# Hybrid decoder layer on one core: mixing loads one step later, chunks begun four units later, down operands four steps ahead

## The chip, the cores and the metric

The kernel runs on one core of a Trainium2 chip. The metric is the device time of one execution in microseconds (us), the median of the runs shown.

## What is computed

One decoder layer, float32, for 2048 positions of width 1024: token mixing, then an MLP of hidden width 4096, each between two RMS norms and added to its input.

```python
S, H = 2048, 4                     # one input; 4 attention heads, 4 mLSTM heads
h = rmsnorm(x, g_mix_pre)
dq, dk, dv, mq, mk, mv, mo, mi, mf = split(h @ w_in)
for blk in range(S // 128):        # differential attention, per head, causal
    s = q[2 maps, 128 rows of blk] @ k[2 maps, all keys up to blk]  # rotary before
    p = softmax(s); p = p[0] - lam * p[1]
    out[blk] = p @ v[keys up to blk]
# mLSTM, recurrent over chunks of positions, per head, with state C and norm n
scores = (qc @ kc.T) * decay_matrix
num = w_inter * (qc @ C) + scores @ vc
C = decay * C + (w * kc).T @ vc
mixed = concat(rmsnorm(attention), rmsnorm(mlstm) * sigmoid(mo)) @ w_out
x = x + rmsnorm(mixed, g_mix_post)
u = square(relu(rmsnorm(x, g_mlp_pre) @ w_up))
return x + rmsnorm(u @ w_down, g_mlp_post)
```

## The kernel before

Five stages follow one another: the input projections (to 560 us), mixing (to 1045), the output projection (to 1300), the up product (to 1880) and the down product (to 2503). A float32 product is made of three matmuls on operands split into a high and a low part. Results of a stage that the next one needs go through DRAM: Kd, Qd and Vd (keys, queries, values), mqkd, Md, Wd, mvd and mod (the mLSTM's inputs), od (the mixed heads), ud (the activations).

**Mixing.** A unit is one head and one block of 128 rows (`units`, 64 of them, 16 to a head). `scores` (L564 on) makes the scores of a unit on PE (L585), DVE adds the mask and finds maxima (L589), ACT takes exponentials (L598); `values` transposes the probabilities (L664), multiplies by V (L669), and DVE scales the result into `o` (L671). After each fourth unit `head_norm` (L675 on) normalises `o` on POOL and ACT and stores it to od by a DMA on POOL's queue (L687). `o` has two places, so that a group's store must have landed before the group after the next writes. K and Q are loaded two units ahead of the unit whose scores are being made, which is itself up to four units ahead (`ahead`); V is loaded two units ahead of `values`.

The mLSTM runs in 16 chunks of 128 positions, each with three stages that are put between the units: `chunk_scores` (transposes L738, scores L747, weighting by E on DVE L749), `chunk_values` (L764, L765, state update L771) and `chunk_norm` (L796 and its store). A chunk has five loads (`chunk_load`: qk, E, two halves of wb, vaug) and a sixth, its gate mog (`chunk_gate`). `chunk_weights` prepares E on POOL and ACT (L725, L727) and wb on POOL (L729). The loop over the units puts the 48 stages in proportion to the work of the units passed. Before: chunks 0 and 1 are loaded and chunk 0 prepared ahead of the loop, later chunks are loaded at the end of `chunk_values` two chunks back.

All these loads go through `load` (L530): SP issues them in the order in which they are written, since `tc.keep_in_program_order` pins the kept instructions of a queue among themselves. A DMA issue waits in SP's queue until the place that it fills is free. Everything that is not kept is ordered by a scheduler at build time.

**The down product.** Seven products of half-size blocks stand for eight (`DOWN_ORDER` 1, 6, 5, 3, 2, 7, 4). Each takes 16 steps; a step is 24 matmuls into eight PSUM banks `pd` (L1034). The operands of a step are made in `operands`: activations `ar` (load L1251), split into `ao` (ACT L1253, DVE L1228), and weights `br` (load L1234), for products 5, 6, 7 and 4 combined out of two to four tiles by DVE (`right`, L1228), then split into `bo` (ACT L1257, DVE L1228). There are 4 places of `ar`, 6 of `ao`, 10 of `br` and 7 of `bo`. At the end of a product `take` copies or adds a bank into `y`; the next product's matmul into that bank waits for it.

Of the kernel before, what the change touches and what calls it, by code (L numbers as in the profile page):

```python
# [15 lines left out]
ALU = mybir.AluOpType  # L16
# [6 lines left out]
NT = 16  # L23
# [9 lines left out]

UP_ORDER = (1, 2, 6, 7, 5, 3, 4)
DOWN_ORDER = (1, 6, 5, 3, 2, 7, 4)
NEAR = (1, 2, 6, 7)

SHAPES = {
# [464 lines left out]
def phase_mix(tc, a, sc, ident, late):  # L503
    nc = tc.nc
    with ExitStack() as ctx:
# [138 lines left out]
        op = pool("op", 2)  # L644
# [5 lines left out]

        def values(u, pd, rz):
            h, qb = units[u]
            load_ahead(1, u + 2)
            if qb % 4 == 0:
                outs[h] = op.tile([128, 4, 128], F32, name="o")
            o = outs[h]
            nb = qb + 1
            pv = psV.tile([128, 128], F32, name="pv")
            for j in range((nb + 3) // 4):
                m = min(4, nb - 4 * j)  # L660
                tp = psT.tile([128, 512], F32, name="tp")
                for i in range(m):
                    b = 4 * j + i
                    nc.tensor.transpose(tp[:, i * 128:(i + 1) * 128], pd[:, b * 128:(b + 1) * 128], ident)  # L664
                pT = ptp.tile([128, 512], F32, name="pT")
                nc.scalar.copy(pT[:, :m * 128], tp[:, :m * 128])
                for i in range(m):
                    b = 4 * j + i
                    nc.tensor.matmul(pv, pT[:, i * 128:(i + 1) * 128], Vs[h, j][:, i, :],  # L669
                                     start=(b == 0), stop=(b == nb - 1))  # L670
            nc.vector.tensor_scalar(o[:, qb % 4, :], pv, rz[:, 0:1], None, op0=ALU.mult)  # L671
            if qb % 4 == 3:
                head_norm(h, qb // 4, o)
# [55 lines left out]
            keep(nc.gpsimd.tensor_tensor(wb, m["qk"][:, 0:2, :], wb, op=ALU.mult))  # L729

        def chunk_scores(c):
            if c + 1 < NT:
                chunk_weights(c + 1)
            m = ms[c]
            qk = m["qk"]
            ktp = psM.tile([128, 512], F32, name="m")
# [16 lines left out]
        def chunk_values(c):  # L753
# [13 lines left out]
            if c < NT - 1:  # L767
                up = psM.tile([128, 512], F32, name="m")
                for h in range(H):
                    hp, r = (h % 2) * 64, h // 2  # L770
# [3 lines left out]
                    nc.vector.scalar_tensor_tensor(C[:, r], C[:, r], dec2[:, r, c:c + 1],  # L774
                                                   up[:, r * 130:(r + 1) * 130], op0=ALU.mult, op1=ALU.add)
            m["ns"] = ns
            if c + 2 < NT:
                chunk_load(c + 2)

        def chunk_norm(c):  # L780
            m = ms.pop(c)
# [8 lines left out]
            for h in range(H):  # L790
# [7 lines left out]
            nc.gpsimd.dma_start(  # L798
                sc["od"][c // 4][c % 4 * 128:c % 4 * 128 + 128, 512:1024].rearrange("p (h v) -> p h v", h=4), mog)
            if c + 2 < NT:  # L800
                chunk_gate(c + 2)

        stages = [chunk_scores, chunk_values, chunk_norm]
        for c in range(2):
            chunk_load(c)
            chunk_gate(c)
        chunk_weights(0)
        N = len(units)
        total = sum(qb + 2 for _, qb in units)
        seen, stage = 0, 0  # L810
        for u in range(N):
            ahead(u)
            seen += units[u][1] + 2
            while stage * total < seen * 48 and stage < 48:
                stages[stage % 3](stage // 3)
                stage += 1
            if u == N - 1:
# [383 lines left out]
def mlp_down(tc, a, sc, out):  # L1201


    nc = tc.nc
    with ExitStack() as ctx:
# [21 lines left out]
        def tt(out, x, y, op):  # L1227
            nc.vector.tensor_tensor(out, x, y, op=op)  # L1228

        def right(i, j):  # L1230
            def load(r, c):
                t = br()
                fb = 2 * j + r - 1
                nc.sync.dma_start(t, a["w_down"][fb * 128:(fb + 1) * 128, (c - 1) * 512:c * 512])  # L1234
                return t

            if i in (1, 2, 3):
                return load(*{1: (1, 1), 2: (2, 1), 3: (2, 2)}[i])
            x, y = load(*((1, 2) if i == 5 else (2, 2))), load(*((1, 1) if i == 5 else (1, 2)))
            tt(x, x, y, ALU.subtract)  # L1240
            if i in (6, 4):
                z = load(1, 1)
                tt(x, x, z, ALU.add)
            if i == 4:
                z = load(2, 1)
                tt(x, z, x, ALU.subtract)
            return x

        def operands(i, j):
# [61 lines left out]
                    nc.vector.scalar_tensor_tensor(t, t, rr, x1[:, sl], op0=ALU.mult, op1=ALU.add)  # L1311
                nc.sync.dma_start(out[rows, sl], t)

        TAIL = 6
        for i in DOWN_ORDER:
            first, last = i in (1, 2, 7), i in (3, 2, 4)
            n = 16 - (TAIL if i == DOWN_ORDER[-1] else 0)
            for j in range(n):
                l, r = operands(i, j)
                for b in range(8):  # L1320
                    step(i, b, l, r, first and j == 0, last and j == 15)
                    if j == 15:
                        take(i, b)
                if i == 7 and j % 2 == 0:
                    load_x1(j // 2, 1)
                    sumsq(j // 2, 1, 1)
                    sumsq(j // 2, 1, 2)
                    finish(j // 2, 1)
                if i == 4 and j < 8:
                    sumsq(j, 2, 2)  # L1330
                if i == 4 and j < 5:
                    load_x1(j, 2)
            if n < 16:
                lr = [operands(i, j) for j in range(n, 16)]
                for b in range(8):
                    for j in range(n, 16):
                        step(i, b, *lr[j - n], False, last and j == 15)
                    take(i, b)
                    sumsq(b, 2, 1)
                    finish(b, 2)  # L1340
                    if b < 3:
                        load_x1(b + 5, 2)


def _constants():
# [62 lines left out]
```

## Time and profile before

| | |
|---|---|
| median of 3 runs | 2508.93 us (2505.14, 2508.93, 2512.16) |
| the profiled execution | 2512.56 us, span 2510.8 us |
| PE busy | 2426.9 us, 97% of the span |
| DVE, ACT, POOL busy | 1467.3, 1061.3 and 468.2 us |
| granted TensorE clock, mean | 0.983 |

A row of the windows view gives the busy time of each engine in a stretch and the clock that PE was granted there (1.00 is 2.4 GHz, 0.50 is 1.2 GHz). In a timeline row the bracket tells how long the engine stood idle before the instruction and what released it. The chain of waits lists the pieces of work, in order of time, on which the end of the program hung. PE is the engine that the other engines feed, so what counts is where PE is idle or slow.

### The profile page before, as it was taken

Reading aid. Unit: us, or ns where it says so; the run is one execution under the profiler, and the core shown is the slowest. Engines: PE = TensorE matmul, PEld = TensorE weight load, DVE = VectorE, ACT = ScalarE, POOL = GpSimd, SP = SyncE. Lnnn points to the kernel's source line nnn. Section 1 sums busy time; section 2 is a strip of 40 time slices with the busy share of each in tenths; the row PEclk is TensorE's granted clock in tenths of the full one; section 3 lists DMA queues with packets and bytes.
Section 4 is the critical chain, followed back from the end, with each engine's and each line's share of the span. In section 5 each row is a group of like instructions: output and inputs, shape, how many; then the busy total and the mean of one; then the engine's idle time right before and its main releaser. Section 6 shows DMA issues by size and latency. Waiting matters only on the chain.

```text
span 2510.8 us, 34565 instructions
## 1 busy us (share of the span) xinstructions
PE 2426.9 (97%) x12030; PEld 2032.6 (81%) x12030; DVE 1467.3 (58%) x3132; ACT 1061.3 (42%) x2103; POOL 468.2 (19%) x756
## 2 busy tenths in 40 slices
PE   8999999998999998999989999999999999999998
PEld 6888889996877787878768888888888888887886
DVE  4474441115887887466676666676664543333885
ACT  7210112324876776544443443443443332332433
POOL 0002222202755646423210000000000000000323
PEclk9999999997999999999999999999999999999999
DMA  9323333226564564255784446734457764444883
GB/s 323 131 76 101 111 112 93 60 84 154 143 139 130 118 153 109 73 179 190 236 316 149 165 150 253 293 140 150 160 200 280 239 206 161 150 150 159 301 284 138
DMA packets 288559, 424.35 MB, mean 169 GB/s; under 512 B 23584, under 2 KB 162224, under 8 KB 286848
## 3 DMA queue, kind: packets, MB, share of 16 engines
q1 hardware_dynamic: 285472, 413.55, 51.3%
q0 software_dynamic: 2912, 8.59, 1.1%
q8 instruction: 95, 1.56, 0.3%
q14 instruction: 80, 0.66, 0.1%
HBM read 283.56 MB, written 138.49 MB: 168 GB/s over the span
## 4 chain that ended last, share of the span: by engine, by line
PE 80%; DVE 8%; DMA 7%; issue 2%; ACT 2%; POOL 1%; SPq 1%; POOLq 0%; DVEq 0%; ACTq 0%
PE pd L1034 16%; PE A L1034 14%; PE B L1034 10%; PE pp L93 7%; PE pp L95 7%; PE pp L94 7%; PE pv L669 4%; DMA br<-in_w_down_dram 4%; PE s L585 4%; PE tp L664 2%; PE po L93 1%; PE po L95 1%; PE po L94 1%; PE m L765 1%; DMA t<-in_x_dram 1%
## 5 line engine op out<-in xcount | busy, mean ns | idle before, releaser
L1034 PE MATMUL pd<-bo,ao 128*128 128x512 f32 x2688 | 614.4, 391 | 6.9 <-DVE y L1228 5.3
L1034 PEld LDWEIGHTS pd<-bo,ao 128*128 128x128 f32 x2688 | 506.3, 189 | 114.8 <-issue 5.0
L1034 PE MATMUL A<-B,w 128*128 128x512 f32 x1536 | 364.8, 393 | 9.8 <-DVE w L1104 4.8
L1034 PEld LDWEIGHTS A<-B,w 128*128 128x128 f32 x1536 | 290.2, 189 | 74.3 <-ACT w L1134 6.9
L93 PE MATMUL pp<-w,xT 128*128 128x512 f32 (+1 forms) x768 | 271.5, 359 | 8.7 <-ACT w L230 7.7
L94 PE MATMUL pp<-w,xT 128*128 128x512 f32 (+1 forms) x768 | 273.1, 356 | 0.0
L1034 PE MATMUL B<-B,w 128*128 128x512 f32 x1152 | 272.2, 389 | 0.0
L95 PE MATMUL pp<-w,xT 128*128 128x512 f32 (+1 forms) x768 | 271.3, 355 | 0.0
L1286 POOL TENSOR_TENSOR y<-y,g 128x512 f32<-128x512 f32 x32 | 49.2, 1561 | 1153.2 <-ACT jk L1280 1089.2
L1034 PEld LDWEIGHTS B<-B,w 128*128 128x128 f32 x1152 | 216.1, 188 | 45.7 <-ACT w L1134 0.9
L1253 ACT CAST ao<-ar 128x1024 fp32r<-128x1024 f32 x112 | 117.7, 1052 | 294.6 <-PE pd L1034 158.7
L1228 DVE TENSOR_TENSOR ao<-ar,ao 128x1024 fp32r<-128x1024 f32 x112 | 139.1, 1243 | 168.0 <-ACT ao L1253 164.3
L1104 DVE TENSOR_TENSOR w<-wr,w 128x512 fp32r<-128x512 f32 x224 | 152.2, 688 | 123.0 <-ACT w L1134 121.7
L585 PE MATMUL s<-K,Q 128*128 128x512 f32 (+3 forms) x640 | 187.0, 405 | 17.3 <-DVE p L589 8.8
L1134 ACT CAST w<-wr 128x512 fp32r<-128x512 f32 x224 | 136.9, 620 | 116.6 <-PE B L1034 106.4
L598 ACT ACTIVATE p<-p,nm 128x128 f32<-128x128 f32 (+15 forms) x128 | 153.8, 1202 | 47.7 <-DVE nm L597 38.2
L669 PE MATMUL pv<-V,pT 128*128 128x128 f32 x1088 | 154.5, 286 | 11.4 <-DVE o L671 8.7
L93 PEld LDWEIGHTS pp<-w,xT 128*128 128x128 f32 x768 | 144.4, 188 | 25.3 <-ACT w L230 8.6
L669 PEld LDWEIGHTS pv<-V,pT 128*128 128x128 f32 x1088 | 142.4, 198 | 22.7 <-DVE o L671 10.0
L95 PEld LDWEIGHTS pp<-w,xT 128*128 128x128 f32 x768 | 144.5, 188 | 15.2
L94 PEld LDWEIGHTS pp<-w,xT 128*128 128x128 f32 x768 | 144.6, 188 | 15.1 <-DVE w L231 0.3
L589 DVE TENSOR_SCALAR_CACHE_REDUCE p<-s 128x512 f32<-128x512 f32 x192 | 129.5, 683 | 28.4 <-PE s L585 22.5
(260 smaller groups left out, 3604.4 us busy)
## 6 DMA issues: line engine op xcount, KB each, us to landing
ud<-u SPq DMA_DIRECT2D x224, 256.0 KB, 2.4
ar<-ud SPq DMA_DIRECT2D x112, 512.0 KB, 3.9
br<-in_w_down_dram SPq DMA_DIRECT2D x224, 256.0 KB, 4.0
wr<-in_w_up_dram SPq DMA_DIRECT2D x128, 256.0 KB, 3.4
Bd<-hl SPq DMA_DIRECT2D x40, 512.0 KB, 4.1
B<-Bd SPq DMA_DIRECT2D x10, 2048.0 KB, 13.3
Q<-Qd SPq DMA_DIRECT2D x128, 128.0 KB, 4.9
raw<-in_xT_dram SPq DMA_DIRECT2D x32, 256.0 KB, 5.0
```

The source lines that it names most:

```text
L93: nc.tensor.matmul(ps, lhs[0], rhs[0], start=first, stop=False)
L94: nc.tensor.matmul(ps, lhs[0], rhs[1], start=False, stop=False)
L95: nc.tensor.matmul(ps, lhs[1], rhs[0], start=False, stop=last)
L585: nc.tensor.matmul(ps[:, :w], Q[:, var, c, qo:qo + 128], Ks[h, j][:, c, 0:w], start=(var == 0), stop=(var == 1))
L589: nc.vector.tensor_scalar(dst, ps[:, :w], 0.0, None, op0=ALU.add, op1=ALU.max, accum_out=mx[:, c, j:j + 1])
L598: nc.scalar.activation(pc[:, :W], pc[:, :W], AF.Exp, bias=nm[:, c:c + 1], accum_out=Z[:, c:c + 1])
L669: nc.tensor.matmul(pv, pT[:, i * 128:(i + 1) * 128], Vs[h, j][:, i, :], start=(b == 0), stop=(b == nb - 1))
L1034: nc.tensor.matmul(ps, l[i], r[j], start=(first and k == 0 and m == 0), stop=(last and k == n - 1 and m == 2), skip_group_check=True)
L1104: self.nc.vector.tensor_tensor(out, x, y, op=op)
L1134: self.nc.scalar.copy(w[:, 0], src)
L1228: nc.vector.tensor_tensor(out, x, y, op=op)
L1253: nc.scalar.copy(l[:, 0], u)
```

## The change

In mixing, V is loaded one unit ahead of `values` where it was two; a chunk's five loads move from the end of `chunk_values` to the end of `chunk_norm` of two chunks back; `chunk_weights` of the next chunk moves from the start of `chunk_scores` to the end of `chunk_values`. The loads of chunks 0 and 1 move into the loop, to units 1 and 3, with the preparation of chunk 0 at unit 3, and the first chunk stage comes four units later (the first four units are 2 + 3 + 4 + 5 = 14 of the 608 that `total` counts). In the down product the operands are made four steps ahead in the written program (in the last product's tail six, as before), and DVE's combinations of `br` tiles are kept in written order.

```diff
         def values(u, pd, rz):
-            load_ahead(1, u + 2)
+            load_ahead(1, u + 1)
...
         def chunk_scores(c):
-            if c + 1 < NT:
-                chunk_weights(c + 1)
...
             m["ns"] = ns
-            if c + 2 < NT:
-                chunk_load(c + 2)
+            if c + 1 < NT:
+                chunk_weights(c + 1)
...
             if c + 2 < NT:
+                chunk_load(c + 2)
                 chunk_gate(c + 2)
...
-        for c in range(2):
-            chunk_load(c)
-            chunk_gate(c)
-        chunk_weights(0)
...
             ahead(u)
             seen += units[u][1] + 2
-            while stage * total < seen * 48 and stage < 48:
+            if u in (1, 3):
+                chunk_load(u // 2)
+                chunk_gate(u // 2)
+            if u == 3:
+                chunk_weights(0)
+            while stage * (total - LEAD) < (seen - LEAD) * 48 and stage < 48:
                 stages[stage % 3](stage // 3)
...
+        def keep(out, x, y, op):
+            tc.keep_in_program_order(nc.vector.tensor_tensor(out, x, y, op=op))
...
-            tt(x, x, y, ALU.subtract)
+            keep(x, x, y, ALU.subtract)
             if i in (6, 4):
                 z = load(1, 1)
-                tt(x, x, z, ALU.add)
+                keep(x, x, z, ALU.add)
             if i == 4:
                 z = load(2, 1)
-                tt(x, z, x, ALU.subtract)
+                keep(x, z, x, ALU.subtract)
...
+        TAIL, AHEAD = 6, 4
+        steps = [(i, j) for i in DOWN_ORDER for j in range(16)]
+        made = []
+        for n, (i, j) in enumerate(steps):
+            tail = n == len(steps) - TAIL
+            while len(made) < min(n + (TAIL if tail else AHEAD + 1), len(steps)):
+                made.append(operands(*steps[len(made)]))
...
-                l, r = operands(i, j)
                 for b in range(8):
-                    step(i, b, l, r, first and j == 0, last and j == 15)
+                    step(i, b, *made[n], first and j == 0, last and j == 15)
```

Three places show what this moves. The lines of the changed kernel are two higher in mixing (L532 for L530) and two to five higher in the down product (L1230 for L1228, L1233 for the kept combinations).

On SP's queue, where mixing begins, before (Kd_64 and Qd_68 hold the keys and queries that units 4 and 5 are the first to read; the two Q groups of four are one tile for units 4 and 5 and one for 6 and 7):

```order
L692 DMA masks<-in_c_masks_dram 128x128
L530 DMA qk<-mqkd 128x4x128
L530 DMA E<-Md 128x4x128
L530 DMA wb<-Wd 64x2x128 x2
L530 DMA vaug_4819<-mvd 128x4x128
L530 DMA mog<-mod 128x512
L530 DMA qk<-mqkd 128x4x128
L530 DMA E<-Md 128x4x128
L530 DMA wb<-Wd 64x2x128 x2
L530 DMA vaug_4820<-mvd 128x4x128
L530 DMA mog<-mod 128x512
L530 DMA K<-Kd_64 64x2x512 x2
```

The same place after the change:

```order
L694 DMA masks<-in_c_masks_dram 128x128
L532 DMA K<-Kd_64 64x2x512 x2
L532 DMA Q<-Qd_68 64x2x256 x4
L532 DMA V<-Vd_71 128x4x128
L532 DMA Q<-Qd_68 64x2x256 x4
L532 DMA qk<-mqkd 128x4x128
L532 DMA E<-Md 128x4x128
L532 DMA wb<-Wd 64x2x128 x2
L532 DMA vaug_4819<-mvd 128x4x128
L532 DMA mog<-mod 128x512
L532 DMA K<-Kd_65 64x2x512 x2
```

Twelve issues of chunks 0 and 1 (qk to mog, six each) stood ahead of that K and Q; now K, Q, V and Q stand first, and the chunks' loads follow.

On PE at the same time, before (the first row is the last of the scores of unit 3, the rows tp are the transposes of units 2 and 3):

```order
L585 MATMUL s<-K,Q 128x512 x2
L738 MATMUL m<-ident,qk 128x128 x2
L747 MATMUL m<-qk 128x128 x2
L664 MATMUL tp<-ident,p 128x128 x3
L747 MATMUL m<-qk 128x128 x2
L664 MATMUL tp<-ident,p 128x128 x4
L764 MATMUL m<-vaug_4819,E 128x130
L765 MATMUL m<-C,wb 128x130
```

And after the change:

```order
L587 MATMUL s<-K,Q 128x512 x2
L666 MATMUL tp<-ident,p 128x128 x3
L587 MATMUL s<-K,Q 128x512
L587 MATMUL s<-K,Q 128x128
L587 MATMUL s<-K,Q 128x512
L666 MATMUL tp<-ident,p 128x128 x4
L587 MATMUL s<-K,Q 128x512
```

Chunk 0's work (L738 to L765) stood ahead of the scores of unit 4; now the scores of unit 4 (the rows L587 with 512, 128, 512) stand between those transposes, and chunk 0's first row comes thirteen rows later than it did, among the scores of unit 5.

On DVE in the down product, where the fifth product ends and its eight banks are taken into `y_17879` (the `br` subtractions are those of the sixth product, br_21247 that of its tenth step; bo_20995 is of its fifth step), before:

```order
L1228 TENSOR_TENSOR ao_20950<-ar_20948,ao_20950 128x1024
L1228 TENSOR_TENSOR bo_20995<-br_20990,bo_20995 128x512
L1228 TENSOR_TENSOR br_21247<-br_21247,br_21249 128x512
L1228 TENSOR_TENSOR y_17879<-y_17879,pd_17871 128x512
L1228 TENSOR_TENSOR ao_20987<-ar_20985,ao_20987 128x1024
L1228 TENSOR_TENSOR y_17879<-y_17879,pd_17872 128x512
L1228 TENSOR_TENSOR bo_21056<-br_21051,bo_21056 128x512
```

And after (bo_20806 is of the sixth product's fourth step, br_20846 of its fifth):

```order
L1230 TENSOR_TENSOR ao_20798<-ar_20796,ao_20798 128x1024
L1233 TENSOR_TENSOR br_20801<-br_20801,br_20803 128x512
L1230 TENSOR_TENSOR bo_20806<-br_20801,bo_20806 128x512
L1230 TENSOR_TENSOR y_17879<-y_17879,pd_17871 128x512
L1230 TENSOR_TENSOR ao_20843<-ar_20841,ao_20843 128x1024
L1233 TENSOR_TENSOR br_20846<-br_20846,br_20848 128x512
L1230 TENSOR_TENSOR y_17879<-y_17879,pd_17872 128x512
```

The take of the first bank stood behind the subtraction for the sixth product's tenth step; now what stands ahead of it is of that product's fourth step, and the subtraction of its fifth step stands between the first take and the second.

## Rows read from the trace of the kernel before

**Rows 1.** the windows view, the two stages that the diff touches: stretch, its length, each engine's busy us (instructions), PE's granted clock, DMA share, GB/s

```profile
560.00:1045.00 485.00, 443.14 (x2832) 368.00 (x2831) 371.85 (x1237) 335.73 (x810) 268.05 (x588) 0.94 0.54 130
1880.00:2503.00 623.00, 614.59 (x2690) 506.27 (x2688) 332.05 (x474) 218.42 (x339) 57.38 (x38) 0.99 0.60 209
```

**Rows 2.** the windows view, the start of mixing in three stretches

```profile
561.00:566.50 5.50, 2.63 (x16) 1.91 (x16) 3.83 (x14) 2.81 (x9) 0.00 (x0) 0.96 0.33 101
566.50:585.00 18.50, 8.41 (x30) 5.37 (x28) 2.97 (x8) 4.84 (x18) 5.06 (x5) 0.50 0.78 184
585.00:603.50 18.50, 18.36 (x61) 13.89 (x62) 8.04 (x32) 4.37 (x10) 1.19 (x1) 0.50 0.77 171
```

**Rows 3.** the timeline of PE there: start us, duration us, what, [idle before <- what ended it]

```profile
564.01 0.44 PE L738 MATMUL m<-ident,qk 128*128 128x128 f32 x2 [2.87 <-DMA qk<-mqkd]
573.89 0.80 PE L764 MATMUL m<-vaug,E 128*128 128x130 f32 x2 [6.63 <-DVE E L749]
585.13 1.41 PE L585 MATMUL s<-K,Q 128*128 128x512 f32 x3 [3.34 <-DMA Q<-Qd]
```

**Rows 4.** the timeline of SP's DMA issues there: start us, time for the issues, what

```profile
560.52 0.34 SPq L692 DMA_DIRECT2D masks<-in_c_masks_dram  x1
572.83 2.51 SPq L530 DMA_DIRECT2D K<-Kd  x2
575.39 4.66 SPq L530 DMA_DIRECT2D Q<-Qd  x4
```

**Rows 5.** the chain of waits, two of its pieces there: start us, us

```profile
566.55 11.61 DMA E<-Md
578.79 6.21 DMA Q<-Qd
```

**Rows 6.** the DMA view, 520 to 640 us: issues, KB of one, median us to landing

```profile
Q<-Qd SPq DMA_DIRECT2D x32, 128.0 KB, 4.4
od<-o POOLq DMA_DIRECT2D x1, 256.0 KB, 2.8
```

**Rows 7.** the windows view, two later stops of PE in mixing, each with the slow stretch behind

```profile
836.00:842.50 6.50, 2.21 (x8) 1.27 (x8) 2.97 (x19) 2.91 (x7) 4.26 (x24) 1.00 0.86 197
842.50:846.00 3.50, 3.40 (x14) 3.31 (x15) 3.50 (x13) 2.48 (x4) 0.84 (x6) 0.51 0.00 0
948.00:952.00 4.00, 1.38 (x5) 0.59 (x4) 4.00 (x10) 2.70 (x7) 3.59 (x4) 0.98 1.09 208
952.00:962.00 10.00, 7.08 (x23) 5.70 (x24) 5.66 (x25) 4.59 (x8) 2.88 (x9) 0.50 0.31 75
```

**Rows 8.** the chain of waits, the store of a finished group of attention rows

```profile
833.40 8.70 DMA od<-o
947.06 8.58 DMA od<-o
```

**Rows 9.** PE's waits by releaser, 1880 to 2503: us in total, times, longest

```profile
PE pd L1034 <- DVE y L1228: 5.3, 2, 4.3
PE pd L1034 <- DVE ao L1228: 1.6, 2, 1.0
```

**Rows 10.** the timeline of DVE where the fifth down product ends

```profile
2318.45 0.69 DVE L1228 TENSOR_TENSOR br<-br,br 128x512 f32<-128x512 f32 x1 [4.28 <-DMA br<-in_w_down_dram]
2319.06 0.68 DVE L1228 TENSOR_TENSOR y<-y,pd 128x512 f32<-128x512 f32 x1
```

**Rows 11.** the windows view, the slow stretch behind that place

```profile
2320.50:2324.00 3.50, 3.50 (x10) 2.71 (x9) 3.50 (x7) 2.69 (x9) 3.43 (x3) 0.51 0.64 222
```

**Rows 12.** groups of instructions in the down products: line, what, count | busy us, mean ns | idle before

```profile
L1228 DVE TENSOR_TENSOR br<-br,br 128x512 f32<-128x512 f32 x112 | 81.4, 731 | 106.0 <-DMA br<-in_w_down_dram 92.7 <-issue 12.5
L1228 DVE TENSOR_TENSOR bo<-br,bo 128x512 fp32r<-128x512 f32 x112 | 79.9, 716 | 4.1 <-ACT bo L1257 4.1
L1257 ACT CAST bo<-br 128x512 fp32r<-128x512 f32 x112 | 68.8, 617 | 61.8 <-DVE br L1228 54.0 <-PE pd L1034 7.7
```

**Rows 13.** the chain of waits, the longest landing of a down weight tile

```profile
2381.47 7.11 DMA br<-in_w_down_dram
```

More of the change, by code (lines that the diff above doesn't have):

```diff
@@ L35 @@
 DOWN_ORDER = (1, 6, 5, 3, 2, 7, 4)
+LEAD = 14
 NEAR = (1, 2, 6, 7)
@@ L1312, in finish @@
                 nc.sync.dma_start(out[rows, sl], t)
-        TAIL = 6
-        for i in DOWN_ORDER:
-            first, last = i in (1, 2, 7), i in (3, 2, 4)
-            n = 16 - (TAIL if i == DOWN_ORDER[-1] else 0)
-            for j in range(n):
-                l, r = operands(i, j)
-                for b in range(8):
-                    step(i, b, l, r, first and j == 0, last and j == 15)
[L1322 to L1337, printed above, removed]
-                    take(i, b)
[L1339 to L1342, printed above, removed]
@@ new lines, in mlp_down @@
+        TAIL, AHEAD = 6, 4
[5 more added lines that the diff above has]
+                made.append(operands(*steps[len(made)]))
+            first, last = i in (1, 2, 7), i in (3, 2, 4)
+            if tail:
+                break
+            for b in range(8):
+                step(i, b, *made[n], first and j == 0, last and j == 15)
+                if j == 15:
+                    take(i, b)
+            if i == 7 and j % 2 == 0:
+                load_x1(j // 2, 1)
+                sumsq(j // 2, 1, 1)
+                sumsq(j // 2, 1, 2)
+                finish(j // 2, 1)
+            if i == 4 and j < 8:
+                sumsq(j, 2, 2)
+            if i == 4 and j < 5:
+                load_x1(j, 2)
@@ L1345, in _constants @@
+        for b in range(8):
+            for j in range(16 - TAIL, 16):
+                step(i, b, *made[j - 16], False, j == 15)
+            take(i, b)
+            sumsq(b, 2, 1)
+            finish(b, 2)
+            if b < 3:
+                load_x1(b + 5, 2)
 def _constants():
```

## The prediction

> **What bounds the kernel now.** I read the windows view by stages first, since PE is busy 97% of the whole span and only its gaps can give anything. In mixing PE is busy 443.14 of 485.00 us, and its mean clock is 0.94; in the down product it is busy 614.59 of 623.00 us [rows 1]. So there are some 42 us of idle time and a slow clock in mixing, and 8.4 us of idle time in the down product. The rest of the program is not touched in what PE does.
>
> Next come the finer windows of mixing's start. From 561.00 to 603.50 PE's busy time is 2.63, 8.41 and 18.36 us, the latter two at a clock of 0.50 [rows 2]. At full clock that is 2.63 + 8.41/2 + 18.36/2 = 16.0 us of work in 42.5 us: 26.5 us are lost, 13.1 as idle time and 13.4 to the clock. It is the largest single loss of the kernel. PE's timeline names the stops: 2.87 us for the load of qk, 6.63 us for E's weighting, 3.34 us for Q [rows 3]. SP's timeline tells why Q is late: after the masks (560.52 + 0.34) twelve loads of chunks 0 and 1 are issued, and K's turn comes at 572.83, Q's at 575.39 [rows 4]. In the chain of waits E's load from 566.55 takes 11.61 us, and the Q piece from 578.79 takes 6.21 us, so it lands at 585.00 [rows 5], which is where PE begins on the scores of unit 4. That half the clock stays on for all of 585.00 to 603.50, with PE busy 18.36 of 18.50 us, is to be kept in mind: idle time costs a second time behind it.
>
> For the later stops of mixing and for the down product I read the chain of waits and PE's waits, below.
>
> **A, the start of mixing: -13 us.** The order shows K and Q of unit 4 directly behind the masks. So K is issued at 560.9 rather than 572.83. K's two issues took 2.51 us, and the Q piece that PE waited for was issued 578.79 - 575.39 = 3.40 us after Q's first [rows 4, 5]; with the same times it goes out at 566.8. Landing in the 6.21 us that it took, it is there at 573.0; in 4.4 us, the median of the Q loads of these 120 us [rows 6], at 571.2. I take 4.4, since E's, wb's and vaug's transfers now come behind it and not ahead. Then the 16.0 us of work follow, chunk 0's part among them, which now has other scores beside it while E is on its way. Of the slow stretches behind later stops in mixing one has 3.40 us of PE time at 0.51 and one 7.08 us at 0.50 [rows 7]; I take the longer, 7.08/2 = 3.5 us lost. 571.2 + 16.0 + 3.5 = 590.7 against 603.5: 12.8, called 13. The ends: Q lands as late as E did, 11.61 us, at 578.4, and the clock stays low for the whole 18.36 us as before (9.2 lost): 578.4 + 16.0 + 9.2 = 603.6, a gain of nothing. On the other side the clock does not fall: 3.5 more, 16.5. DVE must do 3.83 + 2.97 + 8.04 = 14.8 us in the same work [rows 2], less than the 19.5 us that are left, so it does not bound this sum.
>
> **B, the stores of `o`: -3 us.** Two later stops hang on a store, from 833.40 for 8.70 us and from 947.06 for 8.58 us [rows 8]. At the first PE is busy 2.21 of 6.50 us and then 3.40 of 3.50 us at half clock: 4.29 + 0.10 + 1.70 = 6.1 us lost. At the second it is 2.62 + 2.92 + 3.54 = 9.1 us [rows 7]. The store waits in traffic: the DMA share is 0.86 and 1.09 in these rows, and in the quiet start of mixing the same store lands in 2.8 us [rows 6]. The change moves a chunk's five loads by a stage, so that they no longer fall beside these stores; but K, Q and V of the next head still do. The ends are nothing and 6.1 + 9.1 = 15 us; the landing stays nearer to what it was, since most of the traffic stays, and I take 3.
>
> The Trainium skill has a rule against this step. "SBUF — State Buffer", in "SBUF: two separate sides", says that a DMA issued on the POOL queue needs POOL to write its descriptors, and that DVE can shut POOL out of the port it writes through; by it the store waits for DVE and not for traffic, B is 0 and the sum 3 us higher. The trace is divided: DVE is busy 4.00 of 4.00 us beside the second store, but 2.97 of 6.50 beside the first, and both land in about the same time [rows 7, 8].
>
> **C, the down product: -7 us.** PE waits there for `y` twice, 5.3 us in all, 4.3 at the longest, and twice for `ao`, 1.6 us [rows 9]. DVE's timeline shows the long one: the take of the fifth product's first bank (2319.06) stands behind the subtraction for the sixth product's tenth step, which waited 4.28 us for its weight tile [rows 10]. Behind it PE runs 3.50 us at 0.51, 1.7 us more [rows 11]. The new order has nothing further on than the fourth step ahead of that take, whose tiles have long been there. Gone are 4.3 + 1.7 + 1.0, the other `y` wait: 7. The `ao` waits belong to the tail, whose operands are six ahead before and after; I count nothing, so the ends are 0 and -8.6. That the kept subtractions are in order costs nothing as long as a tile lands in time; the case where it doesn't is a rival.
>
> **The other moves: 0.** V comes one unit later. A unit lasts 485/64 = 7.6 us in the mean, and a load like Q lands in 4.4 [rows 1, 6]. A chunk's loads come a stage later, 485/48 = 10.1 us, and two stages still lie between them and their use, 20.2 us against 11.61 for the slowest landing seen [rows 1, 5]. `chunk_weights` moves towards its use by two stages and keeps one, 10.1 us, on engines with room: POOL is busy 268 and ACT 336 of 485 us [rows 1]. The chunks' 48 stages now share 60 units; they are the same instructions. If that cover is gone, the next late thing is E at `chunk_scores`, a wait as in [rows 3].
>
> **Sum.** 2512.56 - 13 - 3 - 7 = 2489.6 for the profiled execution. It stands 3.6 us above the median of the three runs, so I expect 2489.6 - 3.6 = 2486 for the median, 0.9% faster. About 0.3%, 7.5 us, is what a measurement of this kernel can tell from no change.
>
> **The rivals.**
>
> *Late Q* (0.22). Everything at the start of mixing shares the DMA queues, and E's 11.61 us shows what a load can take there. A gives nothing, by its end above, and -3 - 7 = -10 remain: 2499. For it speaks the long half clock behind 585.00; against it that the heavy loads now stand behind Q.
>
> *Given back* (0.15). What mixing gains at its start it loses at the next stop, because DVE, ACT and POOL, at 372, 336 and 268 of 485 us, have their own pace there, and a chunk's stages are denser than before by 64/60. Then only C is left: 2512.56 - 7 - 3.6 = 2502. Against it: PE is the busiest of them, at 443 us with slow stretches [rows 1].
>
> *The store waits for DVE* (0.08). B is 0 whatever the loads do: 2489.
>
> *Slower, by the kept subtractions* (0.07). In the seventh product each step has four weight tiles, and ten places hold two and a half steps. A tile's place comes free when DVE has done its part; so a period of two and a half steps is a landing, three subtractions of 0.73, a cast of 0.62 and a split of 0.72, that is a landing + 3.5 us [rows 12]. PE's step is 614.59/112 = 5.5 us [rows 1]. At the longest landing shown, 7.11 us [rows 13], a step takes 10.6/2.5 = 4.3 and is covered. It decides from a landing of 5.5 x 2.5 - 3.5 = 10.2 us on. At twice 7.11, an estimate, a step takes 7.1 us: 16 steps lose 1.6 each, 25 us. Then 2512.56 - 13 - 3 + 25 - 3.6 = 2518. For it speaks that DVE can no longer go past a late tile; against it that such landings are not seen.
>
> That the change does not do what it says is excluded for A and C by the order; for the weights of the chunks the order moves them too.
>
> **How the numbers follow.** My forecast has 0.48, with a range of its own from 2478 to 2496. Faster by over 0.3%, below 2501.4, are the forecast, late Q and the store's case: 0.48 + 0.22 + 0.08 = 0.78. Given back is the same, 0.15, and the kept subtractions slower, 0.07. With all far ends, 16.5 + 15 + 8.6, the median would be 2469; the range reaches from 2470 to 2505, which takes in all but the slower case and some of the tails.
>
> **What would show it.** A is right if PE's scores of unit 4 begin near 571 in the changed kernel's timeline and the windows up to 603 lose half of what they lost; wrong if PE waits for Q or E as long as before, later. B shows in the landing of the stores and in PE's idle time near 840 and 950. C is right if PE's wait for `y` in the down product is near nothing and no wait for `bo` takes its place; wrong if DVE waits for weight tiles in the seventh product with PE idle behind it. The whole is wrong if mixing does not end some 16 us sooner.

## The result, and the profile after

The changed kernel takes 2490.95 us (median of 4 runs, 2488.46 to 2492.73) against 2509.62 us for the kernel before (4 runs); the ratio is 0.9927, 95% interval 0.9910 to 0.9944. That is 18.7 us less, where 2486 was forecast, inside the range of 2470 to 2505. The profiled execution took 2491.75 us, 20.8 less than the one read before. By stages, each from the first or last instruction of its kind in the two traces:

| stretch | before | after | difference |
|---|---|---|---|
| start to mixing's first transposition | 560.2 | 560.7 | +0.6 |
| mixing, to its last product with V | 482.4 | 473.4 | -9.0 |
| to the first matmul of the up product | 206.8 | 205.3 | -1.5 |
| the up product | 630.8 | 630.9 | 0 |
| the down product on PE | 621.3 | 609.6 | -11.7 |
| to the last busy instruction (the span ends 4.4 us later in both) | 4.9 | 5.7 | +0.8 |

So the total was near the forecast and, in these two traces, the parts were not: 16 us were expected of mixing and 7 of the down product. The windows view of the changed kernel, the two stages that answer to [rows 1]:

```profile
560.00:1045.00 485.00, 441.33 (x2864) 369.65 (x2863) 367.87 (x1236) 333.90 (x811) 278.68 (x604) 0.95 0.56 132
1870.00:2480.00 610.00, 609.88 (x2690) 504.61 (x2689) 338.32 (x472) 220.22 (x336) 57.54 (x37) 1.00 0.60 213
```

In the down product PE is now busy 609.88 of 610.00 us at full clock. No idle time and no slow clock are left to win there. In mixing PE's busy time and clock hardly differ from before; 11 us of this stretch now lie behind mixing's end.

The start of mixing, to be held against [rows 2], in the windows view of the changed kernel:

```profile
561.00:564.00 3.00, 0.70 (x5) 0.27 (x2) 2.93 (x14) 2.95 (x9) 0.00 (x0) 1.00 0.63 210
564.00:568.00 4.00, 0.52 (x3) 0.31 (x3) 1.16 (x4) 0.40 (x2) 0.00 (x0) 0.80 1.13 216
568.00:573.00 5.00, 4.85 (x16) 4.28 (x17) 2.05 (x10) 0.72 (x2) 0.00 (x0) 0.50 1.07 209
573.00:582.00 9.00, 9.00 (x59) 7.87 (x58) 8.05 (x33) 5.73 (x14) 2.62 (x3) 0.99 0.80 134
582.00:588.00 6.00, 2.13 (x15) 1.58 (x13) 3.00 (x10) 5.06 (x19) 0.00 (x0) 0.91 0.92 183
588.00:606.00 18.00, 14.43 (x59) 11.41 (x59) 6.71 (x29) 5.11 (x10) 3.71 (x8) 0.56 0.89 194
```

Idle time is 2.30 + 3.48 + 0.15 + 3.87 + 3.57 = 13.4 us and the clock costs 0.10 + 2.43 + 0.09 + 0.19 + 6.35 = 9.2 us: 22.5 us lost in 45, against 26.5 before. The first 12 us went better than forecast, and then it stopped twice more. PE's timeline of the changed kernel has the four stops (L587 are scores, L666 transposes, L671 products with V):

```profile
564.17 0.52 PE L666 MATMUL tp<-ident,p 128*128 128x128 f32 x3 [2.46 <-DVE p L610]
568.15 1.41 PE L587 MATMUL s<-K,Q 128*128 128x512 f32 x3 [3.46 <-DMA Q<-Qd]
587.60 2.50 PE L587 MATMUL s<-K,Q 128*128 128x512 f32 x6 [3.87 <-DMA Q<-Qd]
596.39 0.79 PE L671 MATMUL pv<-V,pT 128*128 128x128 f32 x2 [3.57 <-DMA V<-Vd]
```

Unit 4's scores begin at 568.15, earlier than the 571.2 of the prediction. But Q of unit 8 lets PE wait 3.87 us at 587.60 and V of units 4 to 7 another 3.57 at 596.39. SP's timeline and the chain of waits show where those loads stood:

```profile
568.64 0.59 SPq L532 DMA_DIRECT2D qk<-mqkd  x1
576.26 4.61 SPq L532 DMA_DIRECT2D Q<-Qd  x4
581.65 0.59 SPq L532 DMA_DIRECT2D qk<-mqkd  x1
587.52 0.43 SPq L532 DMA_DIRECT2D V<-Vd  x1
```

```profile
579.00 7.91 DMA Q<-Qd
587.52 8.83 DMA V<-Vd
```

Q and V now come behind chunk 0's and chunk 1's loads, as Q of unit 4 did before; the DMA share was 0.72 in the first 45 us of mixing before and is 0.90 now, and while PE waits for Q of unit 4, Q of unit 8 and V it is 1.14, 0.91 and 1.11.

The stores of step B, in the chain of waits of the changed kernel, and SP's issues just ahead of the first:

```profile
714.63 9.63 DMA od<-o
943.10 6.87 DMA od<-o
```

```profile
710.43 0.54 SPq L532 DMA_DIRECT2D qk<-mqkd  x1
711.08 0.44 SPq L532 DMA_DIRECT2D E<-Md  x1
714.66 2.23 SPq L532 DMA_DIRECT2D V<-Vd  x1
```

These two are the stores at the first and the third head's end; [rows 8] has the second and the third. At the three ends in order the stores take 9.6 (714.63), 9.6 (828.91, not in the chain) and 6.9 us now, and took 5.2 (718.90), 8.7 and 8.6 us before. The chunk loads that were to leave the heads' ends now come out right ahead of the first of them. At the other two they moved nearer to the store as well: they begin 8 and 10 us ahead of it (820.75 and 932.72), where it was 17 (816.40 and 930.47). The windows view of the changed kernel has the first store in three stretches, and then the stops at the other two ends:

```profile
714.60:718.00 3.40, 2.09 (x8) 0.97 (x6) 3.40 (x11) 2.46 (x8) 1.74 (x3) 1.00 0.19 39
718.00:720.00 2.00, 1.08 (x4) 0.67 (x4) 0.84 (x7) 1.16 (x2) 0.00 (x0) 1.00 0.34 85
720.00:724.30 4.30, 0.00 (x0) 0.00 (x0) 0.00 (x0) 0.00 (x0) 0.00 (x0) 0.50 1.05 313
828.00:837.00 9.00, 5.12 (x27) 3.62 (x25) 7.00 (x30) 5.95 (x17) 4.77 (x9) 0.95 0.89 217
837.00:843.00 6.00, 3.96 (x16) 3.73 (x17) 3.16 (x13) 3.30 (x8) 2.70 (x18) 0.51 1.03 212
943.00:951.00 8.00, 3.33 (x13) 1.96 (x12) 4.61 (x21) 5.14 (x11) 6.77 (x20) 0.86 1.05 244
951.00:957.00 6.00, 6.00 (x31) 5.61 (x30) 5.04 (x20) 3.03 (x5) 4.71 (x14) 0.62 0.57 104
```

Idle time and slow clock cost 8.1 us at the second end and 7.4 at the third, where the prediction reckoned 6.1 and 9.1 for the kernel before. At the first end they cost 10.6 us from 714 to 732, where the kernel before lost 6.0 from 716 to 736. PE's wait for `o` grew, here its line before and after:

```profile
PE pv L669 <- DVE o L671: 8.7, 3, 3.5
```

```profile
PE pv L671 <- DVE o L673: 14.7, 4, 5.3
```

### The profile page after: what moved, and what is told of

Its sections match the earlier page's. It is cut to its first block, busy times and chain, and to the rows that moved or that the text cites. A ratio compares the mean times of both kernels' runs of the same rounds, so it can differ in the third digit from the quotient of the medians.

```text
span 2490.0 us, 34674 instructions
## 1 busy us (share of the span) xinstructions
PE 2411.2 (97%) x12030; PEld 2026.2 (81%) x12030; DVE 1474.2 (59%) x3132; ACT 1063.3 (43%) x2103; POOL 475.6 (19%) x756
## 4 chain that ended last, share of the span: by engine, by line
PE 87%; DVE 4%; DMA 4%; POOL 1%; ACT 1%; issue 1%; SPq 1%; POOLq 0%; ACTq 0%; DVEq 0%
PE pd L1036 24%; PE A L1036 14%; PE B L1036 10%; PE pp L95 7%; PE pp L97 7%; PE pp L96 7%; PE pv L671 4%; PE s L587 3%; PE po L95 2%; PE tp L666 2%; PE po L97 2%; PE po L96 2%; PE m L765 1%; DMA t<-in_x_dram 1%; PE m L764 1%
## 5 line engine op out<-in xcount | busy, mean ns | idle before, releaser
L1036 PE MATMUL pd<-bo,ao 128*128 128x512 f32 x2688 | 609.6, 389 | 0.0
L1230 DVE TENSOR_TENSOR ao<-ar,ao 128x1024 fp32r<-128x1024 f32 x112 | 139.2, 1243 | 218.0 <-ACT ao L1258 212.1
L587 PE MATMUL s<-K,Q 128*128 128x512 f32 (+3 forms) x640 | 184.2, 405 | 13.4 <-DMA Q<-Qd 7.3
L600 ACT ACTIVATE p<-p,nm 128x128 f32<-128x128 f32 (+15 forms) x128 | 153.7, 1201 | 49.4 <-DVE nm L599 38.9
L671 PE MATMUL pv<-V,pT 128*128 128x128 f32 x1088 | 152.8, 285 | 21.5 <-DVE o L673 14.7
L671 PEld LDWEIGHTS pv<-V,pT 128*128 128x128 f32 x1088 | 141.4, 197 | 32.9 <-DVE o L673 14.6
```

Of the source, the lines that this page charges most:

```text
L587: nc.tensor.matmul(ps[:, :w], Q[:, var, c, qo:qo + 128], Ks[h, j][:, c, 0:w], start=(var == 0), stop=(var == 1))
L600: nc.scalar.activation(pc[:, :W], pc[:, :W], AF.Exp, bias=nm[:, c:c + 1], accum_out=Z[:, c:c + 1])
L1036: nc.tensor.matmul(ps, l[i], r[j], start=(first and k == 0 and m == 0), stop=(last and k == n - 1 and m == 2), skip_group_check=True)
```

## The experiments

All runs with their times, ratios to the kernel before and 95% intervals:

| kernel | us | ratio |
|---|---|---|
| down part only | 2501.36 | 0.9972 (0.9960 to 0.9983) |
| mixing part only | 2499.67 | 0.9972 (0.9962 to 0.9982) |
| operands ahead, not kept | 2508.40 | 1.0001 (0.9992 to 1.0010) |
| kept, not ahead | 2498.21 | 0.9967 (0.9954 to 0.9980) |
| late chunks only | 2515.92 | 1.0027 (1.0015 to 1.0038) |
| moved loads only | 2507.00 | 0.9992 (0.9980 to 1.0003) |
| changed kernel, V two ahead | 2504.65 | 0.9983 (0.9974 to 0.9992) |
| changed kernel, three places for o | 2504.76 | 0.9981 (0.9971 to 0.9992) |
| K and Q first | 2503.29 | 0.9971 (0.9961 to 0.9982) |
| changed kernel, gate first | 2492.70 | 0.9933 (0.9920 to 0.9947) |
| changed kernel, chunks at unit 6 | 2500.80 | 0.9956 (0.9942 to 0.9969) |
| changed kernel, store on ACT's queue | 2515.23 | 1.0027 (1.0018 to 1.0037) |

**The two halves.** The down section of the changed kernel in the kernel before, and the reverse.

> Only the down product's part of the change. Theory (the two parts add): the down product alone takes PE's 6.9 us of waits and the slow clock behind them away, 11.7 us as in the changed kernel's trace, so about 2498 against 2509.6, ratio 0.9953. Rival (the gain needs the new order in mixing, since the whole program is ordered at once): under 5 us, 2505 or more.

> Only mixing's part of the change, the down product as before. Theory: mixing gives the 9 us that its stretch of the trace became shorter, and the output projection about 1.5, so about 2500, ratio 0.9958. Rival (mixing's gain is lost again further on): within 4 us of before.

The medians are 7.2 and 8.9 us below before, 16 together, and the product of the ratios, 0.9944, is at the edge of the interval of the whole change. So the parts add, as far as these runs tell. The first lies between its theory (2498) and its rival (2505 or more), the second is as its theory had it. In the trace of the first, the up and the down product together take 1239.4 us on PE, where they took 1252.1: 12.7 less, more than the median shows.

**Which edit does it in the down product.** One kernel has the operands written four steps ahead and no keep, the other the keep alone:

```diff
         def keep(out, x, y, op):
-            tc.keep_in_program_order(nc.vector.tensor_tensor(out, x, y, op=op))
+            nc.vector.tensor_tensor(out, x, y, op=op)
```

```diff
-            tt(x, x, y, ALU.subtract)
+            keep(x, x, y, ALU.subtract)
...
-                tt(x, x, z, ALU.add)
+                keep(x, x, z, ALU.add)
...
-                tt(x, z, x, ALU.subtract)
+                keep(x, z, x, ALU.subtract)
```

> The down part alone, with operands four steps ahead in the written program but the combinations of weight tiles not kept in order. Theory of the prediction (the late tile stood ahead of the take because the scheduler put combinations up to nine steps ahead): without the keep the scheduler puts them far ahead again, so PE's wait for y stays and the time is within 4 us of before, 2506 to 2510. Rival (writing the operands ahead sets the order by itself): 2498 as with both.

> The combinations of weight tiles kept in order, operands written one step at a time as before. Theory of the prediction: the order of the combinations among themselves was nearly the written one before, so keeping them changes little against takes, which are not kept: 2503 to 2510. Rival (the keep is what does it): 2498.

The first came out as the theory had it, the second as the rival. DVE's and PE's timelines of the kernel without the keep are those of [rows 10] again (L1231 is `br`, L1228 `y`):

```profile
2315.82 0.69 DVE L1231 TENSOR_TENSOR br<-br,br 128x512 f32<-128x512 f32 x1 [4.26 <-DMA br<-in_w_down_dram]
2316.43 0.68 DVE L1228 TENSOR_TENSOR y<-y,pd 128x512 f32<-128x512 f32 x1
```

```profile
2317.25 146.28 PE L1034 MATMUL pd<-bo,ao 128*128 128x512 f32 x635 [4.61 <-DVE y L1228]
```

With the keep alone the subtraction runs without waiting and the take of the first bank waits for PE and not PE for it:

```profile
2304.64 0.69 DVE L1231 TENSOR_TENSOR br<-br,br 128x512 f32<-128x512 f32 x1
2308.49 0.69 DVE L1228 TENSOR_TENSOR y<-y,pd 128x512 f32<-128x512 f32 x1 [1.78 <-PE pd L1034]
```

DVE's waits by releaser from 1870 to 2500 us show it for the whole stage, in total, times and longest; without the keep, and in the changed kernel:

```profile
DVE br L1231 <- DMA br<-in_w_down_dram: 98.3, 52, 5.0
```

```profile
DVE br L1233 <- DMA br<-in_w_down_dram: 4.2, 4, 2.6
```

Before it was 92.7 us by [rows 12]. So the keep is the part that works, and writing the operands ahead does nothing that these runs can measure.

**Which edit does it in mixing.** The late begin alone (no loads moved) and the moved loads alone (chunks loaded and begun as before), both with the down product as before:

> The kernel before with the late begin of the chunks alone (loads of chunks 0 and 1 at units 1 and 3, stages four units later); loads of later chunks and of V where they were, the down product as before. Theory (mixing's 9 us come from K and Q of unit 4 standing ahead of the chunks' loads): 7 to 9 us faster, about 2500, ratio 0.9968. Rival (a part of it comes from the moved loads): within 4 us of before.

> The kernel before with the moved loads alone: V one unit ahead, a chunk's five loads at the end of chunk_norm, chunk_weights at the end of chunk_values; chunks begin as before, the down product as before. Theory (step B of the prediction is empty, since in the changed kernel the stores still take 9.63 and 6.87 us): within 3 us of before. Rival (the loads do get out of the stores' way): 3 us or more faster, 2505 or less.

Late chunks alone are 6.8 us slower than before, moved loads alone 2.1 faster, within its interval the same; together they were 8.9 faster. Moved loads alone came out as its theory had it; that late chunks alone are slower neither its theory nor its rival had. The parts of mixing do not add. The next two kernels undo or add a single thing in the changed kernel:

```diff
-            load_ahead(1, u + 1)
+            load_ahead(1, u + 2)
```

```diff
-                outs[h] = op.tile([128, 4, 128], F32, name="o")
+                outs[h] = op.tile([128, 4, 128], F32, name="o", bufs=3)
...
-            oc = op.tile([128, 4, 128], F32, name="oc", bufs=1)
+            oc = mt.tile([128, 4, 128], F32, name="sq")
```

> The changed kernel with V loaded two units ahead again. Theory (V one unit ahead is what put V's load behind chunk 1's at the start: PE waited 3.57 us for it at 596.39, at half clock behind it): 3 to 6 us faster than the changed kernel, about 2486. Rival (the transfers at the start are limited by their volume, so another load is late in its place): 2491, within 2 us of the changed kernel.

> The changed kernel with three places for o instead of two; the room comes from oc, which now shares a place with the squares of chunk_norm. Theory (the stops near 720, 835 and 948 are DVE's wait for a place of o whose store is slow to land): PE's idle time and slow clock there go, 24 us by the trace of the changed kernel at the most, at least half of it, so 2467 to 2479. Rival (the heads' K and Q loads are late there anyway and take the place of the wait): 2487 to 2491, with PE waiting for K or Q at the heads' ends.

Both were 14 us slower than the changed kernel, outside what theory and rival had said. With three places the stops at the second and third head's end did go: PE is busy 8.96 of 10.00 and 6.94 of 7.00 us where the changed kernel stood. But others came elsewhere, at 684 and 807. The windows view of that kernel:

```profile
844.00:854.00 10.00, 8.96 (x65) 7.87 (x64) 9.87 (x41) 9.36 (x30) 4.74 (x10) 1.00 0.77 184
955.00:962.00 7.00, 6.94 (x48) 5.71 (x46) 7.00 (x30) 6.33 (x23) 5.48 (x17) 1.00 0.63 131
679.00:684.00 5.00, 0.98 (x5) 0.37 (x3) 5.00 (x6) 4.24 (x13) 4.91 (x5) 0.88 0.22 79
684.00:692.00 8.00, 7.83 (x25) 5.99 (x26) 5.12 (x14) 1.93 (x6) 4.22 (x11) 0.50 0.05 9
798.00:807.50 9.50, 3.73 (x25) 3.09 (x25) 9.50 (x17) 4.91 (x12) 8.40 (x8) 0.90 0.17 55
807.50:819.00 11.50, 11.50 (x45) 8.99 (x46) 3.92 (x13) 4.12 (x14) 1.18 (x1) 0.50 0.06 11
```

At 798 to 807.50 DVE is busy 9.50 of 9.50 us, and PE, in the timeline, waits for its weighting of E:

```profile
807.44 0.80 PE L764 MATMUL m<-vaug,E 128*128 128x130 f32 x2 [3.14 <-DVE E L749]
```

The order of the instructions is the clue. In these two kernels the scheduler made a new order of all engines, from early in mixing on. So I measured mixing by its own progress: the time from the first transposition to the end of DVE's row `o<-pv,rz` of the 4th, 8th, 16th, 32nd and 64th unit.

| kernel | 4 | 8 | 16 | 32 | 64 | order of PE, DVE and POOL in mixing |
|---|---|---|---|---|---|---|
| before | 47.8 | 67.0 | 140.6 | 257.1 | 482.8 | first |
| down part only | 47.3 | 66.5 | 139.9 | 256.3 | 482.4 | first, row for row |
| ahead, not kept | 47.7 | 66.9 | 139.3 | 256.2 | 480.1 | first, row for row |
| kept, not ahead | 48.5 | 67.7 | 141.4 | 257.7 | 480.8 | first, row for row |
| changed kernel | 19.7 | 57.2 | 135.7 | 253.9 | 473.7 | second |
| mixing part only | 20.2 | 57.7 | 136.2 | 255.5 | 475.0 | second, row for row |
| gate first | 19.9 | 57.6 | 136.1 | 254.3 | 473.4 | second, row for row |
| late chunks only | 19.7 | 56.2 | 138.9 | 259.8 | 485.8 | its own |
| moved loads only | 47.3 | 68.5 | 148.7 | 259.6 | 476.7 | its own |
| V two ahead | 19.7 | 52.8 | 137.9 | 261.3 | 486.5 | its own |
| three places for o | 19.8 | 57.3 | 143.4 | 267.6 | 485.0 | its own |
| K and Q first | 48.2 | 65.9 | 139.0 | 256.3 | 477.8 | its own |
| chunks at unit 6 | 18.6 | 49.4 | 136.1 | 248.6 | 486.8 | its own |
| store on ACT's queue | 19.8 | 57.6 | 140.5 | 266.7 | 495.2 | its own |

Kernels with the same order agree within 2.7 us at the end, kernels with other orders stand anywhere from 473 to 495. Each row is one execution: that of the kernel before lies 2.9 us above its median and that of moved loads only 1.7 below, so small differences between rows prove nothing. One run was made to test this: the gate's load ahead of a chunk's other loads, which moves loads on SP's queue and leaves the other engines' order as it was.

```diff
-                chunk_load(c + 2)
-                chunk_gate(c + 2)
+                chunk_gate(c + 2)
+                chunk_load(c + 2)
```

> The changed kernel with the gate mog loaded ahead of a chunk's other five loads; the order on PE, DVE, ACT and POOL stays the same row for row, only SP's differs. Theory (the times of V two ahead and of three places for o came from the new order that the scheduler made on all engines, not from the loads): with the engines' order held, a move of some loads by one place does nothing, 2489 to 2493. Rival (mixing is that sensitive to the place of a load): 5 us or more to either side.

It came out at 2492.70, within 2 us of the changed kernel, as expected: with the engines' order held, the gate's place on SP's queue did not matter. Two other runs keep the loads' order and have another on the engines. With the store on ACT's queue SP issues the loads of mixing in the changed kernel's order, all 278 of them, and with three places for o the first 265; mixing takes 495.2 and 485.0 us in place of 473.7. So a new order costs this much without any load being moved, though the store's queue and the places of `o` changed as well.

V two ahead did at the start what its theory said: its 8th unit ends at 52.8, 4.4 us ahead of the changed kernel. By the 32nd that was lost.

**The start of mixing by itself.** Two kernels go for step A, one in the kernel before, one in the changed one:

```diff
+        load_ahead(0, 5)
         for c in range(2):
             chunk_load(c)
```

```diff
-LEAD = 14
+LEAD = 27
...
-            if u in (1, 3):
-                chunk_load(u // 2)
-                chunk_gate(u // 2)
-            if u == 3:
+            if u in (3, 5):
+                chunk_load(u // 2 - 1)
+                chunk_gate(u // 2 - 1)
+            if u == 5:
                 chunk_weights(0)
```

> The kernel before with one thing moved: K and Q of units 4 and 5 are loaded ahead of the loads of chunks 0 and 1; chunks begin as before, all else as before. Theory of step A (the loss at the start of mixing is K and Q behind twelve chunk loads): unit 3's attention ends some 10 us sooner, and half of that or more is left at the end, 2500 to 2504. Rival (the transfers of the first 45 us of mixing are limited by their volume, and the chunks' loads now come late for chunk 0's stages, which stand ahead on PE): unit 7 is done no sooner, and the time is within 4 us of before. Second rival (what decides is where the scheduler then puts things in the rest of mixing): the start gains as stated and the end stands anywhere within 8 us.

> The changed kernel with the chunks begun two units later still: loads of chunks 0 and 1 at units 3 and 5, first stage at unit 6. Theory (the first 45 us of mixing are limited by the volume of the loads, 22 us are still lost there, and chunk loads are the part that can wait): PE's waits for Q near 587 and V near 596 shrink, 4 to 8 us faster than the changed kernel, 2483 to 2487. Rival (the order that the scheduler makes of the rest decides): the start is shorter as stated but the end of mixing stands anywhere from 2483 to 2503.

K and Q first gave 2503.29, inside what the theory said, but not in its way: the 4th unit ends at 48.2 against 47.8 and the 8th only 1.1 us sooner. PE's idle time from 561 to 606 us fell from 13.1 to 9.7 us, and the slow clock took it back. The windows view of that kernel:

```profile
563.50:569.50 6.00, 0.52 (x3) 0.31 (x3) 2.44 (x10) 1.76 (x6) 0.00 (x0) 0.85 1.00 210
569.50:605.00 35.50, 32.16 (x105) 24.29 (x106) 13.68 (x52) 12.03 (x33) 5.28 (x5) 0.50 0.84 163
605.00:620.00 15.00, 15.00 (x105) 12.55 (x104) 12.11 (x45) 10.88 (x33) 6.73 (x26) 0.99 0.93 168
```

PE was busy 32.16 of 35.50 us there, all at half clock. That mixing ends 5 us ahead comes from the rest of it, so this run does not show what step A is worth.

With chunks begun at unit 6 the start is better still, 49.4 against 57.2 at the 8th unit and 5.3 us ahead at the 32nd. Then one stop loses it all. In the chain of waits a chunk's E and then Q of the next head follow one another, and PE waits for that Q:

```profile
802.24 9.40 DMA E<-Md
811.65 8.21 DMA Q<-Qd
```

```profile
819.95 0.77 PE L587 MATMUL s<-K,Q 128*128 128x512 f32 x1 [6.26 <-DMA Q<-Qd]
```

That is the rival of this run, and what the second rival of the first had said of the rest of mixing.

**The store's queue.** The stores of `o` on ACT's queue in place of POOL's:

```diff
-            nc.gpsimd.dma_start(
+            nc.scalar.dma_start(
                 sc["od"][g][:, h * 128:(h + 1) * 128].rearrange("(i p) v -> p i v", p=128), o)
```

> The changed kernel with the stores of o issued on ACT's queue instead of POOL's. Theory (a store at the end of a head lands late because K, Q, V and chunk loads fill the DMA engines): away from the heads' ends it lands in some 3 us as before, at the three heads' ends (near 715, 830 and 945) it still takes 6 to 10 us. Rival, by the Trainium skill's rule on DMAs issued by POOL (SBUF - State Buffer, in SBUF: two separate sides): the late stores land in some 3 us too. The time as such tells little, since the engines' order in mixing is made anew: 2485 to 2505.

The kernel takes 2515.23 us, more than the 2485 to 2505 that were expected, and mixing has a new order. Two of the three stores at the heads' ends still take some 7 us, here in its chain of waits, with windows at all three:

```profile
850.52 7.29 DMA od<-o
967.76 6.81 DMA od<-o
```

```profile
724.00:730.00 6.00, 6.00 (x38) 4.73 (x37) 5.07 (x18) 2.64 (x4) 1.26 (x3) 1.00 0.51 140
849.00:859.00 10.00, 1.42 (x5) 0.98 (x6) 1.12 (x9) 3.02 (x7) 2.82 (x4) 0.69 1.07 212
966.00:976.00 10.00, 2.36 (x10) 1.64 (x10) 3.05 (x13) 2.63 (x4) 6.02 (x20) 0.64 1.03 219
```

Around these two DVE is busy only 1.12 and 3.05 of 10.00 us, and the DMA share is 1.07 and 1.03. The store at the first head's end, in a window with a DMA share of 0.51, lands in 3.3 us. So traffic fits as what holds these two stores. It does not fit the first store of the changed kernel, at 714.63: while it is under way the DMA share is 0.19 to 718 and 0.34 to 720, and only then 1.05. DVE is busy all of the 3.40 us to 718 there; but V, issued by SP at 714.66, takes 11.3 us to land as well. What held that one stays open. The Trainium skill's rule ("SBUF — State Buffer", "SBUF: two separate sides") does not decide here: a store that POOL does not issue is late as well.

No experiment points to a version that beats the changed kernel: all that touch mixing's order lose more later than they win, and gate first is equal.

## Why the prediction was right in the total and not in its parts

By its own last sign, "wrong if mixing does not end some 16 us sooner", the prediction failed: mixing's stretch is 9 us shorter. In the two traces the 7 us that mixing did not give are nearly made up by 4.7 more than forecast in the down product and 1.5 ahead of the up product, which nothing had forecast. That the total came so near is in part luck.

**C was right in kind; its size is known roughly.** The named wait was the one that went. 7 us were expected. The two traces differ by 11.7, beyond the -8.6 of the far end; the medians differ by 7.2 (down part only, 4 to 10 by its interval) and 10.4 us (kept, not ahead, 5 to 12). The trace before has a long down product: the four other kernels that leave it as it was (mixing only, late chunks only, moved loads only, K and Q first) take 618.4 to 619.4 us for it, and all kernels with the keep 609.4 to 610.0, so 8 to 10 us less. The term that was mis-sized is "The `ao` waits belong to the tail ...; I count nothing": they went too (1.6 us by [rows 9]), with a slow clock behind them that cost about as much (PE 9.88 us at 0.83 from 2470 to 2480). Some 1.4 us of the 11.7 I can't place. In the changed kernel PE has no wait left. The cause was seen in the right place, the subtraction ahead of the take, but I gave the written steps and the keep as one; the runs show that the keep does it and the steps ahead do not.

**A failed in size.** The Q of unit 4 landed as forecast, or sooner. What failed is "Then the 16.0 us of work follow", with one slow stretch of 3.5 us. The sum put all of the 16.0 us behind 571.2, though PE does 1.2 of them (0.70 + 0.52) before 568; that alone would have made the gain larger. But it took the rest of the stage's loads to be on time, and with a DMA share of 0.90 they were not: two more stops and a second slow stretch (14.43 us at 0.56) came, and 4.0 us were gained in the windows instead of 13. By the table of units 9.8 us are ahead at the 8th unit, when a chunk stage is still owed, and 4.9 at the 16th. What a load no longer waits for, the next load waits for: that was in the rival "late Q" as far as the traffic goes, but for Q of unit 4 and not of unit 8.

**B failed.** The step "so that they no longer fall beside these stores" took the loads' place from the written stage. In the trace they fall right ahead of the store at the first head's end and nearer than before to the other two, and PE's wait for `o` rose from 8.7 to 14.7 us. That the stores wait for traffic and not for DVE fits the two late stores on ACT's queue, and does not fit the one at 714.63.

**"The other moves: 0" failed as well.** V's slack, "A unit lasts 485/64 = 7.6 us in the mean, and a load like Q lands in 4.4", does not hold at the start: the first four units end within 19.7 us, V of units 4 to 7 lands in 8.83 us, and PE waits 3.57 for it. And I argued each moved load by its slack and left out that these edits make the scheduler order mixing anew on all engines. Row for row the same order gave 480 to 483 and 473 to 475 us; other orders, with edits as small as one unit of V's lead, gave 477 to 495. So mixing's 9 us go with the order that this set of edits gave, about 5 of them by the 16th unit, 3 left at the 32nd and the rest after it. What in the second order is better there was not found; that stays open. The rival "given back" was right in part, for some 5 us between the 8th and the 16th unit.

The slower rival, by the kept subtractions, did not show: DVE waits 4.2 us for weight tiles in the whole stage.

## What to carry to other kernels

Where a scheduler orders the program, cost an edit by the order that comes out and not by the edit: compare the rows first, and where a whole stage is made anew, give its time a spread as wide as two orders of the same work differ, here some 20 us of 480. An instruction that waits for a transfer must not be let far ahead on an in-order engine: a keep on the combining instructions took some 90 us of DVE's waits and all of PE's out of the down product. Where a stage's transfers fill the DMA engines, moving one load forward may do little more than name the next one that is late.

## What the runs showed that was not expected

A small instruction of DVE can take many times as long beside POOL. DVE's row for the coefficient `cf`, 128x1, takes 0.22 us in the median of its 62 instances in the changed kernel's mixing and 3.98 at the longest (2.93 in the kernel before). In the kernel with three places for `o` one takes 2.99, and POOL's timeline shows what ran beside it:

```profile
796.18 2.99 DVE L605 SCALAR_TENSOR_TENSOR cf<-Z,nlam,rz 128x1 f32<-128x1 f32 x1
```

```profile
796.38 1.55 POOL L609 TENSOR_TENSOR p<-p 128x640 f32<-128x640 f32 x1
797.88 1.26 POOL L727 TENSOR_TENSOR E<-E,masks 128x512 f32<-128x512 f32 x1
```

It ends at 799.17, just after POOL's two tensor instructions. By the rule of the Trainium skill in the section named above, whichever of the two starts first has the shared port for its whole instruction and the other is shut out. The trace agrees in part: DVE ends only when POOL is through, but its row begins 0.20 us ahead of the first of the two and lasts through both. It is seen here, not tested by a run.

And the half clock can last long under a busy PE: 32.16 us of work in 35.50 us at 0.50 in the kernel with K and Q first, where the changed kernel has 4.85 us at 0.50 and then 9.00 of 9.00 at 0.99 after the same first stop. For the first three microseconds behind the stop both give PE the same rows, scores and transposes; then the kernel with K and Q first gives it chunk 0's transposes and scores, the changed kernel products with V and scores of unit 5. Whether that matters was not tried.
